# Rotary remainder term of the attention scores: two 64-row matmuls in place of two 128-row matmuls

## The chip, the cores and the metric

The kernel runs on one core of one Trainium2 chip. The metric is the time of one execution on the device in microseconds (us); the time before is the median of three runs, 1957.11 us (1955.3 to 1958.13). The engines are named as in the profile: PE is TensorE (matmuls), PEld its weight loads, DVE VectorE, ACT ScalarE, POOL GpSimd, and SP the engine whose queue issues the DMAs.

## The reference

Two batches, `s` (1024 tokens) and `p` (512 tokens), go through the same two layers: a latent attention layer and a gated MLP layer. The change touches only the scores of the attention layer, which has 8 heads:

```python
def one_block(qb):
    qn, qr = qb
    s = (jnp.einsum('bqhd,bkhd->bhqk', qn, k_nope)
         + jnp.einsum('bqhr,bkr->bhqk', qr, k_rope))
    p = jax.nn.softmax(s.astype(jnp.float32) * scale, axis=-1).astype(v.dtype)
    return jnp.einsum('bhqk,bkhd->bqhd', p, v)
```

`qn` and `k_nope` have 128 features per head. The rotary parts `qr` (per head) and `k_rope` (shared by all heads) have 64.

## The kernel before, in words

**Number format.** All large matmuls use a rounded 32-bit type (fp32r). To keep accuracy each operand is split in two: a rounded part ("hi": `qh`, `kh`, `krh`) and the remainder that the rounding left ("lo": `ql`, `kl`, `krl`). A product is then the sum of three matmuls, hi x hi, hi x lo and lo x hi, into one PSUM accumulation. `split` makes the pair: ACT rounds with a copy, DVE subtracts.

**Rotary operands.** The 64 features of the rotary query need only half of the 128 rows of the array. So the tile `qr` of a head holds its hi part in one half of the rows and its lo part in the other (hi in rows 0 to 63 for an even head, in rows 64 to 127 for an odd one). The rotary keys `krh` and `krl` are held twice, once in each half of the rows. One 128-row matmul `qr` x `krh` then gives (hi + lo) x krh, and a second one, `qr` x `krl`, gives (hi + lo) x krl.

**Scores.** `scores(i)` (lines 600 to 615) fills one PSUM tile `s` of 128 x 1024, that is two halves of 512 columns, one for each value of `j2`. For batch `s` the halves are the two key chunks of one block of 128 queries, and there are 8 heads x 8 blocks = 64 calls. For batch `p` they are two query blocks against the one key chunk, and there are 8 x 2 = 16 calls. Each half takes five matmuls of 512 columns, all on line 613: `qh` x `kh`, `qh` x `kl`, `ql` x `kh`, `qr` x `krh`, `qr` x `krl`. Every one has weights of its own (128 x 128, the query side), loaded just before it.

**What follows a score tile.** `softmax1` takes the row maximum on DVE (line 622), a scaled negative of it (line 624), and the exponential on ACT (line 628). `softmax2` normalises on DVE. `transp` makes 8 transposes on PE (line 645), ACT and DVE split the result (lines 150 and 151), and `pv` multiplies with the values on PE in matmuls of 256 columns (lines 145 to 147 with the name `o`).

**Order of work.** `main` writes the order out by hand: for each step `i` it puts the scores of `i`, the transposes of `i - 1`, the `pv` of an earlier step, and pieces that prepare the next head (`p_k`, `p_q`, `p_qr`, `p_v`), so that PE has something to do while DVE and ACT work on the softmax. `first_s` and `first_p` are the pieces ahead of each batch.

**Rotary queries.** `p_qr(p, c)` makes them for a pair of heads and a chunk of 512 tokens, in three pieces. `f1`: nine matmuls, a copy out of PSUM to `qx` on ACT (line 562), and four DMAs on SP's queue that swap 32-row strips into `qs` (line 565). `f2`: two products on DVE with the tables `cos` and `sin` (lines 569 and 570). `f3`: their sum on DVE (line 574), and for each of the two heads a rounding copy on ACT (line 578) and a subtraction on DVE (line 579) into a `qr` tile. It is called 8 times for `s` and 4 times for `p`. `begin` loads the two tables whole, once for each batch, on SP's queue (line 523).

**Buffers.** `tmp` takes a tile of 128 x 512 from a ring of five, which many steps share; a sixth user waits until the first is released.

Of the kernel before, what the change touches and what calls it, by code (L numbers as in the profile page):

```python
# [9 lines left out]
F32 = mybir.dt.float32  # L10
F32R = mybir.dt.float32r
AF = mybir.ActivationFunctionType
ALU = mybir.AluOpType
# [9 lines left out]
C = 512  # L23
# [65 lines left out]
def trunk_kernel(tc, A):  # L89
    nc = tc.nc  # L90
    pe, act, dve, pool_e = nc.tensor, nc.scalar, nc.vector, nc.gpsimd
# [3 lines left out]
    def open_pool(name, side="left", **kw):  # L95
        es_p = ExitStack()
        p = es_p.enter_context(tc.tile_pool(
            name=name, bufs=1, side=side, reuse_waits="tile", **kw))
        opened[name] = es_p
        return p  # L100
# [28 lines left out]
    st = {}  # L129


    def mm_tile(name="mm"):
        return st["ps"].tile([128, C], F32, tag=st["mm"], bufs=4, name=name)

    def big_tile(name="big"):
        return st["ps"].tile([128, 2 * C], F32, tag="big", bufs=2, name=name)

    def tmp(name="tmp", dtype=F32):
        return st["tp"].tile([128, C], dtype, tag="tmp", bufs=5, name=name)

    def mm3(out, terms):

        n = len(terms)
        for i, (lh, ll, rh, rl) in enumerate(terms):
            pe.matmul(out, lh, rh, start=(i == 0), stop=False)  # L145
            pe.matmul(out, lh, rl, start=False, stop=False)  # L146
            pe.matmul(out, ll, rh, start=False, stop=(i == n - 1))  # L147
# [135 lines left out]
    def ksl(k):  # L283
        return slice(k * 128, (k + 1) * 128)
# [228 lines left out]
    def attention(b, n_ch):  # L513

        T = n_ch * C
# [1 line left out]
        nv = 2 * n_ch  # L517

        def begin():
            ap = st["at", b] = open_pool("att" + b)  # L520
            for nm in ("cos", "sin"):
                st[nm] = ap.tile([128, T], F32, name=nm)
                nc.sync.dma_start(out=st[nm], in_=A[nm][:, :T])

        def p_k(h, c):
            def fn():
# [25 lines left out]
        def p_qr(p, c):  # L552
            cc = slice(c * C, (c + 1) * C)

            def f1():
                wh, wl = st["W"].get(("wp", p))
                ps = mm_tile()
                mm3(ps, [(wh[:, ksl(k)], wl[:, ksl(k)],
                          st["lat", b, k][0][:, cc], st["lat", b, k][1][:, cc])
                         for k in range(3)])  # L560
                qx, qs = st["qx"], st["qs"] = tmp("qx"), tmp("qs")
                act.copy(qx, ps)
                for q in range(4):
                    o = (q ^ 1) * 32
                    nc.sync.dma_start(out=qs[o:o + 32], in_=qx[q * 32:q * 32 + 32])

            def f2():
                qx, qs = st["qx"], st["qs"]
                dve.tensor_tensor(out=qx, in0=qx, in1=st["cos"][:, cc], op=ALU.mult)
                dve.tensor_tensor(out=qs, in0=qs, in1=st["sin"][:, cc], op=ALU.mult)  # L570

            def f3():
                qr = st["qx"]
                dve.tensor_tensor(out=qr, in0=qr, in1=st["qs"], op=ALU.add)
                for e in range(2):
                    t = st["at", b].tile([128, C], F32R, tag="qr", bufs=2 + n_ch, name="qr")
                    s, o = 64 * e, 64 * (1 - e)
                    act.copy(t[s:s + 64], qr[s:s + 64])
                    dve.tensor_tensor(out=t[o:o + 64], in0=qr[s:s + 64],
                                      in1=t[s:s + 64].bitcast(F32), op=ALU.subtract)  # L580
                    st["qr", 2 * p + e, c] = t
            return [(f1, ("wp", p)), (f2,), (f3,)]

        def p_v(p, i):
# [15 lines left out]
        def scores(i):  # L600
            h, blk = divmod(i, nb)
            s = big_tile("s")
            kh, kl = st["k", h]
            for j2 in range(2):
                qt, kc = (blk, j2) if n_ch == 2 else (2 * blk + j2, 0)
                c, o = divmod(qt, 4)
                o = ksl(o)
                cc = slice(kc * C, (kc + 1) * C)
                qh, ql = st["q", h, c]
                qr = st["qr", h, c]  # L610
                terms = [(qh, kh), (qh, kl), (ql, kh), (qr, st["krh", b]), (qr, st["krl", b])]
                for j, (l, r) in enumerate(terms):
                    pe.matmul(s[:, j2 * C:(j2 + 1) * C], l[:, o], r[:, cc],  # L613
                              start=(j == 0), stop=(j == 4))
            st["s", i] = s

        ns = 3 - n_ch
# [54 lines left out]
        def put(h, blk, *pc):  # L672
            pieces.setdefault(h * nb + blk, []).extend(pc)

        first = [(begin,)] + [p_k(0, c) for c in range(n_ch)] + [p_q(0, 0)] + p_qr(0, 0)
        first += [p_v(0, i) for i in range(nv)]
        for h in range(HEADS):
            p = h // 2
# [18 lines left out]
            else:  # L697
# [6 lines left out]
                elif nxt:  # L704
                    qr = p_qr(p + 1, 0)
# [4 lines left out]
        def main(weave, filler):  # L710
# [3 lines left out]
            for i in range(n + 2):  # L714
# [3 lines left out]
                if n_ch == 2 and i % 2 == 0:  # L718
                    if i < n:
                        step(lambda i=i: (scores(i), softmax1(i)))  # L720
                    if i >= 1:
                        step(lambda i=i: (transp(i - 1), transp_evac(i - 1)))
                    if i < n:
                        step(lambda i=i: softmax2(i))
                    for p in pc:
                        step(*p)
                elif n_ch == 2:
                    if i < n:
                        step(lambda i=i: (scores(i), softmax1(i), softmax2(i)))
                    if i >= 3:  # L730
                        step(lambda i=i: pv((i - 3) // 2))
                    for p in pc:
                        step(*p)
                    if i <= n:
                        step(lambda i=i: (transp(i - 1), transp_evac(i - 1)))
                else:
                    if i < n:
                        step(lambda i=i: (scores(i), softmax1(i)))
                    if i >= 2:
                        step(lambda i=i: pv(i - 2))  # L740
                    for p in pc:
                        step(*p)
                    if i < n:
                        step(lambda i=i: softmax2(i))
                    if 1 <= i <= n:
                        step(lambda i=i: (transp(i - 1), transp_evac(i - 1)))
# [838 lines left out]
```

## Time and profile before

| | |
|---|---|
| median of three runs | 1957.11 us |
| lowest and highest | 1955.3 and 1958.13 us |
| the profiled execution's own time | 1961.11 us |
| its span, first to last instruction | 1959.3 us |
| mean granted TensorE clock | 0.992 of full speed |

The profile is of one execution. Busy time of an engine is summed over its instructions. Matmuls overlap in the records: each is recorded for longer than the distance from its start to the start of the next, so what a matmul costs in a stream is read from the distance between starts.

### The profile page before, as it was taken

The page shows a single profiled execution, that of the slowest core. Times are in us where ns is not written, and L with a number is a line of the kernel's source. Part 1 is how long each engine was busy: PE and PEld are TensorE (multiplying, and loading weights), DVE is VectorE, ACT ScalarE, POOL GpSimd, SP SyncE. Part 2 cuts the span into 40 slices and gives each one's busy share as a digit, 9 for nine tenths or more (in the row PEclk, how much of TensorE's full clock was granted, in tenths as well). Part 3 has the DMA queues.
Part 4 walks back from the last instruction along what each step waited for, and adds up shares of the span by engine and source line. Part 5 has one row for each costly group of instructions (what it writes and reads, how often), then busy time and mean ns, then how long its engine had stood idle before and what let it go on. Part 6 is the DMA issues. An engine that isn't in the chain of part 4 may idle for free.

```text
span 1959.3 us, 26497 instructions
## 1 busy us (share of the span) xinstructions
PE 1918.5 (98%) x10226; PEld 1698.4 (87%) x10226; DVE 1286.6 (66%) x1958; ACT 889.0 (45%) x1382; POOL 144.3 (7%) x99
## 2 busy tenths in 40 slices
PE   8999999999998999999999999989999999999998
PEld 6888888888887888888789999978778999998887
DVE  7443777777777787549658777665655666656443
ACT  5322545444543555325544554543544454545321
POOL 5200000000011000223000000002000000000111
PEclk9999999999999999999999999999999999999999
DMA  5211000000127211676646655555575555546443
GB/s 162 86 38 57 29 13 22 17 28 17 38 68 244 85 50 60 216 257 196 201 161 226 209 193 183 173 191 186 161 245 192 177 177 183 169 135 222 168 160 103
DMA packets 118638, 269.41 MB, mean 138 GB/s; under 512 B 11888, under 2 KB 40048, under 8 KB 118512
## 3 DMA queue, kind: packets, MB, share of 16 engines
q1 hardware_dynamic: 118512, 267.73, 41.5%
q8 instruction: 80, 1.31, 0.3%
q14 instruction: 46, 0.38, 0.1%
HBM read 198.74 MB, written 65.01 MB: 135 GB/s over the span
## 4 chain that ended last, share of the span: by engine, by line
PE 88%; DVE 6%; DMA 3%; issue 1%; ACT 1%; POOL 0%; SPq 0%; POOLq 0%; DVEq 0%; ACTq 0%
PE s L613 9%; PE mm L145 7%; PE mm L146 7%; PE mm L147 7%; PE X L996 6%; PE X L997 6%; PE X L998 6%; PE mm L1257 4%; PE mm L1259 4%; PE mm L1258 4%; PE pst L645 3%; PE Z L997 3%; PE Z L996 3%; PE Z L998 3%; PE sv L1131 2%; PE o L146 2%
## 5 line engine op out<-in xcount | busy, mean ns | idle before, releaser
L63 ACT CAST w_hi<-w_raw 128x1024 fp32r<-128x1024 f32 (+3 forms) x267 | 260.6, 977 | 391.2 <-PE mm L146 102.4
L64 DVE TENSOR_TENSOR w_lo<-w_raw,w_hi 128x1024 fp32r<-128x1024 f32 (+3 forms) x267 | 303.6, 1137 | 191.5 <-ACT w_hi L63 190.8
L225 POOL TENSOR_TENSOR acc<-acc,sq 128x512 f32<-128x512 f32 x70 | 119.4, 1708 | 1444.7 <-ACT sq L223 851.2
L1257 PE MATMUL mm<-sh,w_hi 128*128 128x512 f32 (+1 forms) x416 | 155.9, 376 | 5.3 <-ACT sh L1177 5.3
L1259 PE MATMUL mm<-sh,w_lo 128*128 128x512 f32 (+1 forms) x416 | 156.1, 375 | 0.0
L1258 PE MATMUL mm<-sl,w_hi 128*128 128x512 f32 (+1 forms) x416 | 156.1, 375 | 0.0
L628 ACT ACTIVATE p<-s,sm 128x1024 f32<-128x1024 f32 (+1 forms) x96 | 93.2, 974 | 103.7 <-DVE sm L624 103.6
L150 ACT CAST pth<-pst 128x512 fp32r<-128x512 f32 x160 | 86.5, 590 | 67.4 <-PE pst L645 65.4
L145 PE MATMUL mm<-h_hi,w_hi 128*128 128x512 f32 x288 | 114.3, 397 | 1.0 <-ACT rbc L328 0.9
L146 PE MATMUL mm<-h_lo,w_hi 128*128 128x512 f32 x288 | 112.6, 391 | 0.0
L147 PE MATMUL mm<-h_hi,w_lo 128*128 128x512 f32 x288 | 112.5, 391 | 0.0
L622 DVE TENSOR_REDUCE sm<-s 128x1 f32<-128x1024 f32 (+1 forms) x80 | 97.4, 1217 | 19.5 <-PE s L613 19.4
L151 DVE TENSOR_TENSOR ptl<-pst,pth 128x512 fp32r<-128x512 f32 x160 | 104.6, 681 | 8.4 <-ACT pth L150 8.3
L1006 ACT COPY t<-X 128x384 f32<-128x384 f32 (+1 forms) x88 | 44.5, 511 | 126.9 <-PE X L998 126.0
L1257 PEld LDWEIGHTS mm<-sh,w_hi 128*128 128x128 f32 x416 | 78.9, 190 | 19.5 <-ACT sh L1177 5.7
L1258 PEld LDWEIGHTS mm<-sl,w_hi 128*128 128x128 f32 x416 | 78.9, 190 | 14.1 <-DVE sl L1178 0.2
L146 PE MATMUL o<-ptl,vh 128*128 128x256 f32 x320 | 91.1, 285 | 0.0
L1259 PEld LDWEIGHTS mm<-sh,w_lo 128*128 128x128 f32 x416 | 78.9, 190 | 14.0
L147 PE MATMUL o<-pth,vl 128*128 128x256 f32 x320 | 91.0, 284 | 0.0
L996 PE MATMUL X<-gbh,w_hi 128*128 128x384 f32 x256 | 86.0, 336 | 5.0 <-DVE uo L1096 5.0
L145 PE MATMUL o<-pth,vh 128*128 128x256 f32 x320 | 90.2, 282 | 0.0
L996 PE MATMUL X<-gah,w_hi 128*128 128x384 f32 x256 | 86.9, 339 | 0.0
(292 smaller groups left out, 5107.1 us busy)
## 6 DMA issues: line engine op xcount, KB each, us to landing
w_raw<-wbo SPq DMA_DIRECT2D x50, 512.0 KB, 3.4
w_raw<-wug SPq DMA_DIRECT2D x48, 512.0 KB, 4.4
w_raw<-sv SPq DMA_DIRECT2D x32, 512.0 KB, 3.5
su<-su SPq DMA_DIRECT2D x32, 512.0 KB, 4.4
w_raw<-su SPq DMA_DIRECT2D x32, 512.0 KB, 4.9
w_raw<-wa SPq DMA_DIRECT2D x25, 512.0 KB, 3.6
w_raw<-wv SPq DMA_DIRECT2D x24, 512.0 KB, 3.5
v2d<-c SPq DMA_DIRECT2D x48, 256.0 KB, 2.6
```

The costliest lines, as they stand in the source:

```text
L63: self.nc.scalar.copy(hi[:, :n], raw[:, :n])
L64: self.nc.vector.tensor_tensor(out=lo[:, :n], in0=raw[:, :n], in1=hi[:, :n].bitcast(F32), op=ALU.subtract)
L145: pe.matmul(out, lh, rh, start=(i == 0), stop=False)
L146: pe.matmul(out, lh, rl, start=False, stop=False)
L147: pe.matmul(out, ll, rh, start=False, stop=(i == n - 1))
L613: pe.matmul(s[:, j2 * C:(j2 + 1) * C], l[:, o], r[:, cc], start=(j == 0), stop=(j == 4))
L996: pe.matmul(ps, lh, rh, start=first, stop=False, skip_group_check=True)
L997: pe.matmul(ps, lh, rl, start=False, stop=False, skip_group_check=True)
L998: pe.matmul(ps, ll, rh, start=False, stop=last, skip_group_check=True)
L1257: pe.matmul(ps, wh[:, ksl(kk)], sh, start=(k == 0), stop=False)
L1258: pe.matmul(ps, wh[:, ksl(kk)], sl, start=False, stop=False)
L1259: pe.matmul(ps, wl[:, ksl(kk)], sh, start=False, stop=(k == 15))
```

## The change

- `scores`: each half keeps four 128-row matmuls; the fifth, `qr` x `krl`, becomes a 64-row matmul of the hi rows of the query with the same rows of `krl`. The first half uses rows 0 to 63, the second rows 64 to 127. Both are put at the end of the call, one right after the other. The product of the two remainders (lo x krl) is no longer computed.
- `p_qr`: for each pair of heads and chunk a new tile `qrx` holds the hi parts in the opposite halves of the rows (two more rounding copies on ACT in `f3`), so that a head's hi part is there in both halves.
- `cos` and `sin` are no longer loaded whole in `begin`; `f1` loads the 512 columns it needs, into a buffer of their own for `s` and into two tiles of the shared `tmp` ring for `p`.

```diff
         def begin():
-            ap = st["at", b] = open_pool("att" + b)
-            for nm in ("cos", "sin"):
-                st[nm] = ap.tile([128, T], F32, name=nm)
-                nc.sync.dma_start(out=st[nm], in_=A[nm][:, :T])
+            st["at", b] = open_pool("att" + b)
...
                 mm3(ps, [(wh[:, ksl(k)], wl[:, ksl(k)],
                           st["lat", b, k][0][:, cc], st["lat", b, k][1][:, cc])
                          for k in range(3)])
+                for nm in ("cos", "sin"):
+                    st[nm] = tmp(nm) if n_ch == 1 else st["at", b].tile(
+                        [128, C], F32, tag=nm, bufs=1, name=nm)
+                    nc.sync.dma_start(out=st[nm], in_=A[nm][:, cc])
                 qx, qs = st["qx"], st["qs"] = tmp("qx"), tmp("qs")
...
-                dve.tensor_tensor(out=qx, in0=qx, in1=st["cos"][:, cc], op=ALU.mult)
-                dve.tensor_tensor(out=qs, in0=qs, in1=st["sin"][:, cc], op=ALU.mult)
+                dve.tensor_tensor(out=qx, in0=qx, in1=st["cos"], op=ALU.mult)
+                dve.tensor_tensor(out=qs, in0=qs, in1=st["sin"], op=ALU.mult)
 
             def f3():
                 qr = st["qx"]
                 dve.tensor_tensor(out=qr, in0=qr, in1=st["qs"], op=ALU.add)
+
+                x = st["qrx", p, c] = st["at", b].tile([128, C], F32R, tag="qrx", bufs=n_ch, name="qrx")
                 for e in range(2):
                     t = st["at", b].tile([128, C], F32R, tag="qr", bufs=2 + n_ch, name="qr")
                     s, o = 64 * e, 64 * (1 - e)
                     act.copy(t[s:s + 64], qr[s:s + 64])
+                    act.copy(x[o:o + 64], qr[s:s + 64])
                     dve.tensor_tensor(out=t[o:o + 64], in0=qr[s:s + 64],
                                       in1=t[s:s + 64].bitcast(F32), op=ALU.subtract)
...
             kh, kl = st["k", h]
+            last = []
             for j2 in range(2):
...
-                terms = [(qh, kh), (qh, kl), (ql, kh), (qr, st["krh", b]), (qr, st["krl", b])]
+                terms = [(qh, kh), (qh, kl), (ql, kh), (qr, st["krh", b])]
                 for j, (l, r) in enumerate(terms):
                     pe.matmul(s[:, j2 * C:(j2 + 1) * C], l[:, o], r[:, cc],
-                              start=(j == 0), stop=(j == 4))
+                              start=(j == 0), stop=False)
+
+                rows = slice(64 * j2, 64 * j2 + 64)
+                hi = qr if j2 == h % 2 else st["qrx", h // 2, c]
+                last.append((s[:, j2 * C:(j2 + 1) * C], hi[rows, o], st["krl", b][rows, cc]))
+            for out, l, r in last:
+                pe.matmul(out, l, r, start=False, stop=True)
             st["s", i] = s
```

## Rows read from the trace of the kernel before

**Rows 1.** The page's list of engines: busy us, share of the span, instructions.
```profile
PE 1918.5 (98%) x10226; PEld 1698.4 (87%) x10226; DVE 1286.6 (66%) x1958; ACT 889.0 (45%) x1382; POOL 144.3 (7%) x99
```

**Rows 2.** Busy time by stretch of the span: attention of `s`, then of `p`.
```profile
core 0: us, PE busy (x) PEld busy (x) DVE busy (x) ACT busy (x) POOL busy (x), PEclk, DMA share, GB/s
186.00:560.00 374.00, 370.85 (x2285) 327.12 (x2285) 286.94 (x502) 192.96 (x339) 8.86 (x6) 1.00 0.09 26
...
680.00:785.00 105.00, 105.00 (x635) 92.19 (x634) 87.12 (x162) 57.22 (x125) 0.00 (x0) 1.00 0.18 57
```

**Rows 3.** What PE waited for, 180 to 790 us: total us, times, longest us.
```profile
PE ps_n L179 <- ACT sh L150: 2.1, 1, 2.1
PE ps_n L180 <- DVE sl L151: 1.9, 2, 1.6
PE pst L645 <- DVE sm L624: 1.6, 2, 1.3
PE s L613 <- ACT p L628: 1.3, 2, 1.0
```

**Rows 4.** The chain that ended last, 180 to 260 us: start us, us, what.
```profile
by line: PE s L613 36.7%; PE pst L645 12.5%; PE mm L147 10.8%; PE mm L146 10.4%; PE mm L145 10.4%; PE o L147 6.0%; PE o L146 6.0%; PE o L145 5.9%; issue 1.1%; ACT p L628 0.5%; ACTq L562 0.0%
...
233.93 2.31 PE s L613 x10
```

**Rows 5.** Instructions of the tile `s` on line 613: duration ns min/median/max, first and last start.
```profile
L613 PE MATMUL s<-kh,qh x160: 387/393/501, 189.1 to 774.5; 128*128 128x512 f32 x160
...
L613 PE MATMUL s<-krl,qr x160: 387/389/398, 193.3 to 775.5; 128*128 128x512 f32 x160
```

**Rows 6.** Timeline of one score tile and its end: start us, us, engine, instruction.
```profile
239.04 0.39 PE L613 MATMUL s<-kh,qh 128*128 128x512 f32 x1
239.04 0.19 PEld L613 LDWEIGHTS s<-kl,qh 128*128 128x128 f32 x1
239.26 0.39 PE L613 MATMUL s<-kl,qh 128*128 128x512 f32 x1
...
241.08 0.39 PE L613 MATMUL s<-krl,qr 128*128 128x512 f32 x1
241.08 0.19 PEld L145 LDWEIGHTS o<-pth,vh 128*128 128x128 f32 x1
241.31 0.28 PE L145 MATMUL o<-pth,vh 128*128 128x256 f32 x1
241.42 0.28 PE L146 MATMUL o<-ptl,vh 128*128 128x256 f32 x1
```

**Rows 7.** Timeline where transposes are followed by a score tile.
```profile
232.89 1.04 PE L645 MATMUL pst<-ident,p 128*128 128x128 f32 x8
...
233.66 0.19 PEld L613 LDWEIGHTS s<-kh,qh 128*128 128x128 f32 x1
233.68 0.48 PE L613 MATMUL s<-kh,qh 128*128 128x512 f32 x1
...
234.00 0.39 PE L613 MATMUL s<-kl,qh 128*128 128x512 f32 x1
```

**Rows 8.** Instructions of the tiles `qr` and `cos`: duration ns min/median/max.
```profile
L578 ACT CAST qr<-qx x24: 607/618/627, 191.6 to 750.5; 64x512 fp32r<-64x512 f32 x24
...
L523 SPq DMA_DIRECT2D cos<-cos x2: 372/496/621, 168.2 to 628.5; - x2
...
DMA to landing us min/median/max: 3.9/4.2/8.0
```

**Rows 9.** Timeline of the first `p_qr` and the first score tile.
```profile
178.17 0.33 SPq L55 DMA_DIRECT2D w_raw<-wh  x1
...
184.18 2.41 SPq L565 DMA_DIRECT2D qs<-qx  x4
...
189.06 0.68 DVE L569 TENSOR_TENSOR qx<-qx,cos 128x512 f32<-128x512 f32 x1
...
191.57 1.26 ACT L578 CAST qr<-qx 64x512 fp32r<-64x512 f32 x2 [1.71 <-DVE qx L574]
...
192.73 0.39 PE L146 MATMUL mm<-lat0l,w_hi 128*128 128x512 f32 x1
...
192.97 0.50 PE L613 MATMUL s<-krh,qr 128*128 128x512 f32 x1
```

## The prediction

> **What bounds the kernel now.** I read the page's list of engines first: PE is busy for 98% of the span, DVE for 66%, ACT for 45% [rows 1]. That is an average over stages, so the next view is busy time by stretch, for the two stretches in which scores are computed. In the attention of `s` PE is busy for 370.85 of 374 us, DVE for 286.94 and ACT for 192.96; in that of `p` PE is busy for 105 of 105 us, DVE for 87.12 and ACT for 57.22 [rows 2]. The granted clock is 1.00 in both, and DMA is nearly idle (0.09 and 0.18). The view of PE's waits says the same from the other side: between 180 and 790 us the four longest entries come to 6.9 us together, and two of those are norms outside the scores [rows 3]. Last, the chain that ended last: between 180 and 260 us it runs almost wholly over PE, 36.7% of it on line 613 [rows 4]. So a microsecond that PE's stream loses in these stretches is a microsecond of the time, as long as DVE keeps up.
>
> What one matmul of that stream costs is not its recorded 389 ns [rows 5] but the distance between starts. The tile of 239.04 us is followed by the first `pv` matmul at 241.31, so ten matmuls take 2.27 us; the chain puts another tile at 2.31 [rows 6, 4]. That is 0.227 to 0.231 us each; I use 0.23. The weights of a matmul begin to load when the matmul before it starts (239.04 for both) and are recorded for 0.19 us, less than 0.23, so in this stream loads are hidden [rows 6].
>
> **Part 1: two matmuls become a pair.** Line 613 has five forms of 160 matmuls, 800 in all, or ten for each of 80 score tiles [rows 5]. The count stays ten, but the last two are on different halves of the rows and write different halves of `s`, so they can run at the same time. If they overlap fully, each tile loses one slot: 80 x 0.23 = **18.4 us**. If they don't overlap, it loses nothing.
>
> A page agrees that they can: the Trainium skill, "TensorE: Matmul & The Clock Gate", Part 3, says that matmuls on different row groups run concurrently and start about 4 ns apart. By it alone the term would be an estimated 80 x (0.23 - 0.004) = 18.1 us. Every matmul of this trace is 128*128, so no row here bears it out.
>
> **Part 2: the array changes its shape twice per tile**, from 128 rows to 64 before the pair and back after it. Nothing in the trace changes shape, so this is bounded from rows. Below: nothing, if the change is made on the fly (a gain is excluded: no work is removed by it). Above: everything that is overlapped in the stream becomes visible. That is the tail of a matmul, recorded 0.39 us less the 0.23 to the next start, 0.16 us [rows 6]; and a weight load that could not run ahead. The price of the latter has a row: after eight transposes, which are too short to cover a load, the first score matmul is followed by the second after 0.32 us (233.68 to 234.00) and not 0.23, and its weights began to load only 0.02 us before it, so an uncovered load costs 0.09 us [rows 7]. Upper bound for one change of shape: 0.16 + 0.09 = 0.25 us, for two 0.50.
>
> I take **0.09 us for both together**: one load that cannot run ahead. The transposes' row is the nearest, since it is the only place where the stream goes from one kind of matmul to another, and it shows an uncovered load but no gap of a whole tail. Only one because two loads have to be made ready ahead of the pair, while after it the next load has the pair's whole 0.23 us to hide in. Whether that one load falls before the pair or between its halves makes no difference to the sum. Price: 80 x 0.09 = 7.2 us; bounds 0 and 80 x 0.50 = 40 us.
>
> **Part 3: two more rounding copies per `p_qr`.** 12 calls, 24 copies of 64 x 512; the existing ones take 0.618 us each [rows 8], so ACT gets 24 x 0.618 = 14.8 us, on an engine that is busy about half of these stretches [rows 2]. Behind them on ACT stand the exponentials and the roundings after the transposes, which PE reaches one step later. I count nothing. If that cover were gone, the place is `p`, where `f3` falls between two exponentials three times after the first: 3 x 2 x 0.618 = 3.7 us at most. The first tile of `s` is the other tight place. There the copy for `qr` starts at 191.57 and PE takes up `qr` at 192.97, 0.24 after the matmul before, so without a gap [rows 9]. Four copies instead of two end at about 191.57 + 4 x 0.62 = 194.05, and the pair, now the last of the tile, would come seven slots after 192.97 at the earliest, at 194.6: hidden.
>
> **Part 4: the tables.** Four loads go, 24 of 256 KB come, in `f1` ahead of the four `qs` DMAs on SP's queue. SP issues in some 0.5 us and a table lands in 4.2 [rows 8]. In the first call SP is free from 178.5 on, the `qs` DMAs go at 184.18 and DVE uses `cos` at 189.06 [rows 9]: a load issued by 179.5 lands by 184. The buffer of `s` is released a whole head-half earlier. For `p` the ring of five now lends four tiles from `f1` to `f2`. In the attention of `p` no other piece takes from the ring; ahead of it the slots belonged to steps PE has long passed. A weight load queued behind a table on SP has the DMA engines nearly to itself (0.09 and 0.18) [rows 2]. Nothing counted; bounded by one landing for each batch, 2 x 4.2 = 8.4 us.
>
> **Part 5: who is next.** DVE gets no work. With 64 x 0.14 = 9 us less its share in `s` becomes 286.94 / 365 = 79%, in `p` 87.12 / 102.8 = 85%. It does not become the bound.
>
> **Sum.** 18.4 - 7.2 = **11.2 us** less. The profiled execution takes 1961.1 us, 4.0 above the median of the runs; it would become 1949.9, and the median 1957.1 - 11.2 = **1946 us**.
>
> **The rivals.** *The array empties at each change of shape (slower).* The 64-row matmuls wait until the last 128-row one has left, and the next 128-row one until the pair has left. Two tails are 2 x 0.16 = 0.32 us against 0.23 saved: 0.09 x 80 = +7.2 us, 1964 us. If the loads wait as well, 2 x 0.25 - 0.23 = 0.27 us, +21.6, 1979 us. It decides from the point where the two changes together cost more than 0.23. For it: a tail of 0.16 is in flight whenever the next matmul starts, and no row shows the array being switched under it. Against it: transposes and matmuls follow each other with less than 0.1 us extra [rows 7]. The Trainium skill speaks for it: "TensorEngine Tiling (Array Packing)", Tiling Modes, says that a change of tiling mode, as against a change of tile, drains TensorE. It gives no time for that, and the trace has no such change to compare. Because of that rule I give this rival 0.28.
>
> *The pair brings nothing (the change doesn't do what it says).* The second half starts only when the first has ended, because its weights load late or because another matmul comes between: around the first tile the matmuls of `p_q` do stand between those of one tile (192.73 before 192.97) [rows 9]. Then the gain is 0 and cheap changes of shape leave 1957 us. The same time comes out if the pair overlaps and the two changes cost just about 0.23. Together 0.17.
>
> *The changes of shape cost nothing.* The whole 18.4 us, 1939 us. This is the near end of the forecast's case, not a case apart.
>
> **How the numbers follow.** The forecast's case is a pair that overlaps with changes of shape that cost at most 0.18 us together; it holds 0.55, and its own range is 1938 to 1953 us. A measurement of this kernel can tell about 0.2% from no change, 3.9 us, or 0.05 us per tile. So faster is 0.55, same 0.17, slower 0.28. The range reaches from the whole saving, 1938, past the two tails, 1964, to 1968, which takes in the late copies (3.7) on top; the case in which loads wait too, about one in ten, is left out.
>
> **What would show it.** Right: on line 613 eight 128*128 matmuls and two of 64 rows per tile, the latter starting well under 0.2 us apart, and a tile from first start to the next work in some 2.1 us; PE still busy for 98% or more of both stretches. The price of the changes is the distance from the last 128-row start to the first 64-row start, beyond 0.23, and from the second 64-row start to what follows, beyond 0.23. Parts 3 and 4 are wrong if PE waits for `qr`, `qrx` or `s` by more than the few us of now. The prediction is wrong if the two distances exceed 0.23 us in sum, or if the 64-row starts lie 0.23 apart.

## The result and the profile after

The changed kernel takes 1967.6 us (median of five runs, 1965.4 to 1973.1), the kernel before 1957.1. The ratio is **1.0057, with a 95% interval of 1.0045 to 1.0069**: slower by 0.57%, some 11 us. A second measurement on another chip, below, gave 1.0048 (1.0032 to 1.0065). The forecast was 1946 us with 0.55 on faster. The measured time lies just inside the top of the range, on the side that had 0.28.

The profiled execution of the changed kernel took 1970.89 us, its span is 1969.1 us. PE still bounds the two stretches. These are the page's list of engines and the busy time of the stretches 186 to 560 and 680 to 785 us (busy us and instructions of PE, PEld, DVE, ACT, POOL, then granted clock, DMA share, GB/s), to be read beside [rows 1, 2]:

```profile
PE 1927.2 (98%) x10226; PEld 1675.4 (85%) x10226; DVE 1289.6 (65%) x1958; ACT 903.5 (46%) x1406; POOL 144.1 (7%) x99
```

```profile
186.00:560.00 374.00, 371.44 (x2243) 304.50 (x2243) 283.56 (x490) 198.31 (x348) 6.90 (x5) 1.00 0.12 36
680.00:785.00 105.00, 105.00 (x617) 86.82 (x616) 90.07 (x165) 65.75 (x137) 0.00 (x0) 1.00 0.21 65
```

The number of matmuls is the same, 10226. PE is as full as before and got fewer of them done in the same 374 us: 2243 instead of 2285. Its weight loads were busy for 304.50 us instead of 327.12. An engine that is always "busy" and does less is the sign to look at distances between starts. The granted clock did not move. PE's waits between 180 and 800 us are those of before [rows 3], with no wait for `qr`, `qrx` or a table near the top:

```profile
PE ps_n L179 <- ACT sh L150: 3.2, 1, 3.2
PE ps_n L180 <- DVE sl L151: 2.1, 2, 1.8
PE s L618 <- ACT p L639: 1.6, 2, 1.4
```

The instructions of the tile `s` show that the change does what it says, 80 and 80 matmuls of 64 rows (64*128 stands for the rows and columns of the array that are used), and that their recorded durations say nothing of the cost (498 ns against 389):

```profile
L618 PE MATMUL s<-krh,qr x160: 387/389/499, 193.2 to 785.4; 128*128 128x512 f32 x160
...
L625 PE MATMUL s<-krl,qr x80: 492/498/503, 194.6 to 785.7; 64*128 64x512 f32 x80
...
L625 PE MATMUL s<-krl,qrx x80: 492/498/502, 194.6 to 785.7; 64*128 64x512 f32 x80
```

Now the timeline around one pair, from the last 128-row matmul of the tile into the `pv` that follows (start us, us, engine, instruction, idle before):

```profile
230.59 0.39 PE L618 MATMUL s<-kh,ql 128*128 128x512 f32 x1
230.59 0.19 PEld L618 LDWEIGHTS s<-krh,qr 128*128 128x128 f32 x1
230.81 0.39 PE L618 MATMUL s<-krh,qr 128*128 128x512 f32 x1
231.13 0.18 PEld L625 LDWEIGHTS s<-krl,qr 64*128 64x128 f32 x1 [0.35 <-issue]
231.13 0.50 PE L625 MATMUL s<-krl,qr 64*128 64x512 f32 x1
231.13 0.18 PEld L625 LDWEIGHTS s<-krl,qrx 64*128 64x128 f32 x1
231.14 0.49 PE L625 MATMUL s<-krl,qrx 64*128 64x512 f32 x1
231.56 0.19 PEld L145 LDWEIGHTS o<-pth,vh 128*128 128x128 f32 x1 [0.24 <-issue]
231.56 0.39 PE L145 MATMUL o<-pth,vh 128*128 128x256 f32 x1
231.79 0.28 PE L146 MATMUL o<-ptl,vh 128*128 128x256 f32 x1
231.90 0.28 PE L147 MATMUL o<-pth,vl 128*128 128x256 f32 x1
```

Read it by starts. The pair overlaps completely: its two starts lie 0.01 us apart. But the load for it does not begin at 230.81, when the matmul before it starts, as the loads of the plain stream do. It begins at 231.13, 0.32 us later: one slot of 0.23 (the distance between two starts in the plain stream) and 0.09 more. The pair then holds PE from 231.13 to 231.56, 0.43 us instead of 0.23. And the first `pv` matmul is followed after 0.23 us, where the next ones are 0.11 to 0.12 apart. I read the same on the way out as on the way in: the stream stops for 0.09 us beyond the slot, and only then does the load of the new shape begin, which nothing covers (0.10 to 0.11 us). Experiment 3 separates the two parts. What fills the 0.09 us the records do not show: the ends of matmuls are modelled, and the pair starts at 231.13, before the recorded end of the last 128-row matmul (230.81 + 0.39 = 231.20). All 80 pairs show these distances, with medians of 0.32 from the last 128-row start to the pair and 0.43 from the pair to what follows.

So one visit to the 64-row shape, that is the way into it and back, costs 0.09 + 0.20 + 0.10 = **0.39 us** beyond its slots (the last term is a first `pv` distance of 0.22 at the median against 0.12). Before transposes the last part is smaller: the eight transposes take 0.85 us to the next matmul (237.76 to 238.61 in the rows below) and not the 0.79 of [rows 7], so 0.35 in all. In 31 of the 80 tiles transposes follow, in 49 a `pv` or another matmul. The saved slot is 0.23: (49 x 0.39 + 31 x 0.35) / 80 - 0.23 = 0.145 us per tile, 80 x 0.145 = **11.6 us**. By the ratios the loss is 11.2 us in the first measurement and 9.4 in the second.

```profile
237.01 0.39 PE L618 MATMUL s<-krh,qr 128*128 128x512 f32 x1
...
237.33 0.50 PE L625 MATMUL s<-krl,qrx 64*128 64x512 f32 x1
...
237.76 1.09 PE L656 MATMUL pst<-ident,p 128*128 128x128 f32 x8
...
238.61 0.49 PE L145 MATMUL mm<-lat0h,w_hi 128*128 128x512 f32 x1
```

The same as a sum over the whole attention: for each PE start in the timeline, the distance to the next start, added up by kind of instruction from the first score matmul to the last (us).

| | before | changed |
|---|---|---|
| score matmuls on 128 rows, not ahead of a pair | 191.73 (800) | 135.27 (560) |
| score matmuls on 128 rows ahead of a pair | | 25.66 (80) |
| score matmuls on 64 rows | | 34.63 (160) |
| `pv`, 256 columns (`o`) | 111.33 | 114.52 |
| transposes (`pst`) | 62.76 | 63.85 |
| other matmuls of 512 columns (`mm`) | 184.00 | 186.20 |
| first to last score matmul, all kinds | 586.62 | 596.87 |

The scores themselves take 195.56 us instead of 191.73, though a slot per tile is gone. `pv` and the transposes behind them pay another 4.3. That is 8.1 us, so the price of 11.6 overstates what reaches the time by some 3.5; where these are made up I did not trace. The `mm` matmuls add 2.2 us, of which 1.6 lie between the two attentions (564.37 to 668.38 us before, 571.43 to 677.02 here), where no pair stands; that stretch takes 103.4 to 107.7 us in the profiles of this case.

### The profile page after: what moved, and what is told of

Same layout as the page of the kernel before. It is cut to its first block, busy times and chain, and to the rows that moved or that the text cites. A ratio compares the mean times of both kernels' runs of the same rounds, so it can differ in the third digit from the quotient of the medians.

```text
span 1969.1 us, 26560 instructions
## 1 busy us (share of the span) xinstructions
PE 1927.2 (98%) x10226; PEld 1675.4 (85%) x10226; DVE 1289.6 (65%) x1958; ACT 903.5 (46%) x1406; POOL 144.1 (7%) x99
## 4 chain that ended last, share of the span: by engine, by line
PE 84%; DVE 7%; DMA 5%; ACT 1%; issue 1%; POOL 0%; SPq 0%; DVEq 0%; POOLq 0%; ACTq 0%
PE s L618 7%; PE mm L145 6%; PE mm L147 6%; PE X L1007 6%; PE mm L146 6%; PE X L1009 6%; PE X L1008 6%; PE mm L1268 4%; PE mm L1269 4%; PE mm L1270 4%; PE pst L656 3%; PE Z L1008 3%; PE Z L1007 3%; PE Z L1009 3%; PE sv L1142 2%; PE o L145 2%
## 5 line engine op out<-in xcount | busy, mean ns | idle before, releaser
L145 PE MATMUL o<-pth,vh 128*128 128x256 f32 x320 | 94.8, 296 | 0.0
```

## The experiments

Ten kernels were run. The diffs are against the changed kernel; differences in us are ratios times about 1958 us.

**1. The side parts alone.** `scores` as before, the extra copies and the table loads kept.

```diff
-                terms = [(qh, kh), (qh, kl), (ql, kh), (qr, st["krh", b])]
+                terms = [(qh, kh), (qh, kl), (ql, kh), (qr, st["krh", b]), (qr, st["krl", b])]
...
-            for out, l, r in last:
-                pe.matmul(out, l, r, start=False, stop=True)
```

> The changed kernel with the scores of before: all ten matmuls of a tile on 128 rows, but the two more rounding copies and the table loads per 512 columns stay. Theory (the whole loss is in the two changes of shape around each pair): as before, 1957 us within 4. Rival (the copies, the table loads or the tighter ring of temporary tiles make the loss): about 1967 us, with waits of PE for qr, cos or temporaries.

Measured 1.0008 (0.9996 to 1.0021), +1.6 us with an interval that reaches zero. So the loss is not in the 24 copies, the 24 loads or the ring of temporary tiles; they cost at most 4 us.

**2. The pair without its overlap.** Both 64-row matmuls on rows 0 to 63.

```diff
-                rows = slice(64 * j2, 64 * j2 + 64)
-                hi = qr if j2 == h % 2 else st["qrx", h // 2, c]
+                rows = slice(0, 64)
+                hi = qr if h % 2 == 0 else st["qrx", h // 2, c]
```

> Both 64-row matmuls use rows 0 to 63, so they cannot overlap. Theory (the overlap works and is worth one slot of 0.23 us per tile): 80 x 0.23 = 18 us above the changed kernel, 1986 us, or up to 80 x 0.34 = 27 us, 1995 us, if the second one's weights cannot load ahead either. Rival (the pair brings nothing, the halves run one after another anyway): equal to the changed kernel, 1967 us.

Measured 1.0126 (1.0111 to 1.0141), 1986.5 us: 13.5 us above the changed kernel by the ratios, 16.9 us by the two profiled attentions (613.72 us from the first to the last score matmul against 596.87), where 18 was expected. A tile in the timeline:

```profile
231.25 0.39 PE L618 MATMUL s<-krh,qr 128*128 128x512 f32 x1
231.56 0.29 PEld L625 LDWEIGHTS s<-krl,qr 64*128 64x128 f32 x2 [0.35 <-issue]
231.57 0.73 PE L625 MATMUL s<-krl,qr 64*128 64x512 f32 x2
232.22 0.19 PEld L145 LDWEIGHTS o<-pth,vh 128*128 128x128 f32 x1 [0.36 <-issue]
```

The visit now lasts 0.65 us (231.57 to 232.22), the 0.43 of the overlapped pair and one slot; its median is 0.66. The overlap is real and worth its slot; the second load of the same rows hides behind the first matmul. The entry is unchanged, 0.32.

**3. Three pairs in one visit.** Six 128-row matmuls, then three pairs: nine slots again.

```diff
-                terms = [(qh, kh), (qh, kl), (ql, kh), (qr, st["krh", b])]
+                terms = [(qh, kh), (qh, kl), (ql, kh)]
...
-                last.append((s[:, j2 * C:(j2 + 1) * C], hi[rows, o], st["krl", b][rows, cc]))
-            for out, l, r in last:
-                pe.matmul(out, l, r, start=False, stop=True)
+                last.append((s[:, j2 * C:(j2 + 1) * C], hi[rows, o],
+                             [st[nm, b][rows, cc] for nm in ("krh", "krl", "krl")]))
+            for j in range(3):
+                for out, l, r in last:
+                    pe.matmul(out, l, r[j], start=False, stop=(j == 2))
```

> Per tile six 128-row matmuls and then three pairs of 64 rows, in one visit to the 64-row shape (hi x krh, hi x krl, hi x krl once more; the product lo x krh is left out, so only the time counts). Nine slots as in the changed kernel. Theory (the price is per change of shape, not per pair): a further pair costs 0.23 us like the 128-row slot it replaces, so 1967 us within 5; if within the shape loads cannot run ahead, 2 x 0.11 x 80 = 18 us more, 1985 us. Rival (a pair of 64 rows is slow by itself, 0.43 us against 0.23): 2 x 0.20 x 80 = 32 us more, 1999 us.

Measured 1.0074 (1.0059 to 1.0089), 1975.6 us: 3 us above the changed kernel by the ratios. One visit:

```profile
230.38 0.39 PE L618 MATMUL s<-kh,ql 128*128 128x512 f32 x1
230.70 0.18 PEld L627 LDWEIGHTS s<-krh,qr 64*128 64x128 f32 x1 [0.35 <-issue]
230.70 0.49 PE L627 MATMUL s<-krh,qr 64*128 64x512 f32 x1
...
230.81 0.19 PEld L627 LDWEIGHTS s<-krl,qr 64*128 64x128 f32 x1
230.81 0.19 PEld L627 LDWEIGHTS s<-krl,qrx 64*128 64x128 f32 x1
231.04 0.39 PE L627 MATMUL s<-krl,qr 64*128 64x512 f32 x1
...
231.27 0.39 PE L627 MATMUL s<-krl,qr 64*128 64x512 f32 x1
...
231.60 0.19 PEld L145 LDWEIGHTS o<-pth,vh 128*128 128x128 f32 x1 [0.37 <-issue]
```

This separates the two parts of the price. The first pair starts its successor after 0.34 us (230.70 to 231.04): its own load of 0.11, uncovered, and a slot. The next distance is 0.23 (231.04 to 231.27): within the shape both loads run ahead (230.81), and a pair costs exactly a slot. The last is 0.33: a slot and 0.10 until the old shape is through. So the price is per change of shape, not per pair. The pairs also go back and forth between the two halves of `s` at 0.23, so it is not this order, new with the change, that costs. The score matmuls sum to 197.1 us here against 195.6 in the changed kernel, and `pv` to 119.53 against 114.52, with waits for DVE that the changed kernel does not show (2.0 us for `ptl` on line 146). In the profiles the attention is thus some 6 us longer, not 3.

**4. The same matmuls in two visits.** One pair after the first half's three 128-row matmuls, two at the end.

```diff
+            for j2 in range(2):
+                (qh, kh, ql, kl, o, cc), out = last[j2][:2]
+                for j, (l, r) in enumerate([(qh, kh), (qh, kl), (ql, kh)]):
+                    pe.matmul(out, l[:, o], r[:, cc], start=(j == 0 and j2 == 0), stop=False)
+                for j in ((0,), (1, 2))[j2]:
+                    for e, (_, out, l, r) in enumerate(last):
+                        pe.matmul(out, l, r[j], start=(j == 0 and e == 1), stop=(j == 2))
```

> The same 128-row and 64-row matmuls as the run with three pairs, in another order: one pair after the first half's three 128-row matmuls, two pairs at the end, so two visits to the 64-row shape per tile in place of one. Theory: one visit more costs 0.09 (entry) + 0.20 (in the visit beyond a slot) + 0.10 (after it) = 0.39 us, 80 x 0.39 = 31 us above the run with three pairs. Rival (price per pair): no difference from the run with three pairs.

Measured 1.0185 (1.0168 to 1.0202), 1998.5 us: 22 us above experiment 3. The added visit, between two halves:

```profile
231.68 0.39 PE L623 MATMUL s<-kh,ql 128*128 128x512 f32 x1
...
232.00 0.50 PE L626 MATMUL s<-krh,qr 64*128 64x512 f32 x1
...
232.43 0.50 PE L623 MATMUL s<-kh,qh 128*128 128x512 f32 x1
...
232.77 0.39 PE L623 MATMUL s<-kl,qh 128*128 128x512 f32 x1
```

0.32, 0.43 and 0.34 us where three slots would take 0.69: 0.40 us for one visit. The distances of all score matmuls sum to 228.06 us against 197.1, 31 us more as expected; `pv` gives 4 us back (115.51 against 119.53), and its waits for DVE are gone from PE's list: probably the slower tile leaves DVE more time. The rest of the difference to the measured 22 us I did not trace.

**5 to 7. Fewer visits, the order alone, another place.** These ran beside the changed kernel on one chip.

> The changed kernel itself, beside the next three on one chip. Theory and rivals alike: some 10 to 11 us above the kernel before, ratio about 1.0055.

> In batch s the scores of two tiles are computed together and their two pairs put in one visit to the 64-row shape, so 32 visits for 64 tiles; batch p keeps 128-row remainders (no visits). Theory (0.35 to 0.39 us per visit, 0.46 us saved by its two pairs): 32 x (0.46 - 0.37) = 3 us below the run with the same order and no visits, and 13 us below the changed kernel if the order costs nothing. Rival (each pair has a price of its own): 64 x 0.15 = 10 us above the run with the same order.

> The order of the grouped run, with every remainder on 128 rows: no visit. It prices the order alone. If transposes find their softmax done in time, as before, 1957 us within 4; if not, PE waits for DVE or ACT and both grouped runs are slower by the same amount.

> The pair is put first in each tile instead of last. About 55 of 80 tiles follow transposes and there pay for an uncovered load already before the change (0.32 between the first two starts instead of 0.23). Theory (each change of shape is an emptying of about 0.09 us and an uncovered load of about 0.11): those tiles pay the load at entry once, not twice, so 55 x 0.31 + 25 x 0.39 = 27 us of price instead of 30, some 3 us below the changed kernel. Rival (the price is one lump per change, wherever it stands): equal to the changed kernel within 1.

The edit of the grouped run, in short (the order control puts `krl` back among the 128-row terms):

```diff
-        def scores(i):
+        def scores(*ii):
...
-                        step(lambda i=i: (scores(i), softmax1(i)))
+                        step(lambda i=i: (scores(i, i + 1), softmax1(i)))
...
-                        step(lambda i=i: softmax2(i))
+                        step(lambda i=i: (softmax1(i + 1), softmax2(i)))
...
-                        step(lambda i=i: (scores(i), softmax1(i), softmax2(i)))
+                        step(lambda i=i: softmax2(i))
```

The changed kernel again, without an edit: 1.0048 (1.0032 to 1.0065). The order alone: 1.0040 (1.0026 to 1.0054), +7.8 us, so the order was not free. Grouped: 1.0085 (1.0068 to 1.0102), 9 us above the order alone where 3 us below was expected. The visit is as forecast, two pairs for one price, 0.32 into it and 0.34 + 0.32 through it:

```profile
230.98 0.39 PE L623 MATMUL s<-krh,qr 128*128 128x512 f32 x1
231.30 0.49 PE L631 MATMUL s<-krl,qr 64*128 64x512 f32 x1
...
231.64 0.39 PE L631 MATMUL s<-krl,qr 64*128 64x512 f32 x1
...
231.96 1.09 PE L661 MATMUL pst<-ident,p 128*128 128x128 f32 x8
```

The score matmuls do take 4.9 us less than in the order control (183.76 against 188.69). But with the pairs at the very end both tiles are ready only then, the softmax of the first starts 1.8 us later (its maximum on DVE starts 4.39 us after the first score matmul at the median, against 2.61 in the order control), and PE waits more further on. PE's waits in the grouped run, then in the order control:

```profile
PE o L146 <- DVE ptl L151: 9.2, 10, 2.2
PE s L623 <- ACT p L644: 3.4, 1, 3.4
PE o L145 <- ACT pth L150: 3.1, 7, 0.7
```

```profile
PE s L622 <- ACT p L637: 6.3, 5, 2.2
...
PE o L145 <- ACT pth L150: 1.1, 3, 0.6
```

`pv` and the transposes together grow by 11.3 us against the control (126.18 + 71.21 against 119.00 + 67.06). So the theory's price held and its saving was lost to new waits. The total, 9 us above the order alone, is close to the 10 us of the rival. Taken alone it would have spoken for a price per pair; the timeline and the sum of the score matmuls speak against it.

The pair first in the tile:

```diff
+                out = s[:, j2 * C:(j2 + 1) * C]
+                pe.matmul(out, hi[rows, o], st["krl", b][rows, cc], start=True, stop=False)
+                last.append((out, o, cc, [(qh, kh), (qh, kl), (ql, kh), (qr, st["krh", b])]))
+            for out, o, cc, terms in last:
+                for j, (l, r) in enumerate(terms):
+                    pe.matmul(out, l[:, o], r[:, cc], start=False, stop=(j == 3))
```

It measured 1.0092 (1.0073 to 1.0112), 9 us above the changed kernel, where 3 us below was expected. Two things went against it. After transposes the entry costs more, not less: 0.96 us from the first of eight transposes to the pair against 0.79 to a 128-row matmul [rows 7], 0.17 more, and the pair still pays its load (0.43 to the next start).

```profile
236.22 1.03 PE L654 MATMUL pst<-ident,p 128*128 128x128 f32 x8
...
237.18 0.50 PE L619 MATMUL s<-krl,qr 64*128 64x512 f32 x1
237.61 0.19 PEld L623 LDWEIGHTS s<-kh,qh 128*128 128x128 f32 x1 [0.24 <-ACT pth L150]
```

And the first tile can no longer begin without the rotary operands: the first score matmul starts at 192.5 us instead of 189.3. With the attention itself 3.2 us longer than in the changed kernel beside it (601.07 against 597.86) this makes 6.4 of the 9 us. So "0.09 to empty" holds after matmuls of 512 columns; after transposes it is about twice that, and why is open.

**8. One visit for two tiles in the old order.** The first tile of two does its own pair and opens the second tile's accumulation with the second pair.

```diff
+            if i % 2 == 0:
+                st["s", i], st["s", i + 1] = big_tile("s"), big_tile("s")
...
+                    pe.matmul(out, l[:, o], r[:, cc], start=(j == 0 and i % 2 == 0),
+                              stop=(j == 3 and i % 2 == 1))
+            if i % 2 == 0:
+                for e in range(2):
+                    for j2 in range(2):
+                        c, o, cc, out = half(i + e, j2)
+                        rows = slice(64 * j2, 64 * j2 + 64)
+                        hi = st["qr", h, c] if j2 == h % 2 else st["qrx", h // 2, c]
+                        pe.matmul(out, hi[rows, o], st["krl", b][rows, cc], start=(e == 1), stop=(e == 0))
```

> The order of the work as in the kernel before; the first tile of each two computes its own pair at its end and, in the same visit, the pair with which the second tile's accumulation begins. 40 visits for 80 tiles, and no softmax waits for a later tile. Theory (0.35 us per visit where transposes follow, up to 0.39 otherwise; 0.46 saved by the two pairs): 40 x (0.46 - 0.37) = 4 us below the run with the side parts alone, so about 1956 us, within 0.2% of the kernel before, and 12 us below the changed kernel. Rival (a price per pair, or waits of the softmax as in the grouped run): 10 us above the kernel before.

Measured **0.9985 (0.9976 to 0.9994)**, 1956.5 us against 1960.1 beside it: by the ratios 2.9 us faster than the kernel before, and 12 to 14 us faster than the changed one in its two measurements. It is the fastest version that keeps the whole product of the changed kernel. A shared visit:

```profile
237.49 0.40 PE L620 MATMUL s<-krh,qr 128*128 128x512 f32 x1
237.82 0.50 PE L628 MATMUL s<-krl,qrx 64*128 64x512 f32 x1
...
238.16 0.39 PE L628 MATMUL s<-krl,qrx 64*128 64x512 f32 x1
...
238.48 1.09 PE L658 MATMUL pst<-ident,p 128*128 128x128 f32 x8
```

The two pairs take 0.66 us (237.82 to 238.48), two slots and 0.20. The score matmuls sum to 187.05 us (144.79 + 12.92 + 29.34), 4.7 less than before. So the price of a visit is borne out, but that the total came out as worked out is in part luck. The transposes (65.1 us against 62.8), `pv` (112.3 against 111.3) and the other matmuls take the 4.7 us back, and the profiled executions need the same 586.4 us from the first score matmul to the last (189.07 to 775.47 before, 189.44 to 775.82 here). Where the 2.9 us arise is open: the profiled spans differ after the last score matmul, where no edit is, 1183.8 us before against 1179.6 here, and the other profiles of this case have 1180.0 to 1186.1 there.

**9. No pair at all.** The eight 128-row matmuls alone.

```diff
-                              start=(j == 0), stop=False)
+                              start=(j == 0), stop=(j == 3))
...
-            for out, l, r in last:
-                pe.matmul(out, l, r, start=False, stop=True)
```

> The changed kernel without the hi x krl term: eight 128-row matmuls per tile, no pair, no change of shape (the term is left out of the result). It prices a slot of PE in the whole kernel. Theory (PE bounds these stretches, a slot of 0.23 us is 0.23 us of the time): 80 x 2 x 0.23 = 37 us below the run with the side parts alone, about 1922 us. Rival (DVE or ACT take over as PE's stream gets shorter): clearly less, 20 us or so, with waits of PE for the softmax.

Measured 0.9863 (0.9846 to 0.9880), 27 us less than before and 28 less than the side parts alone, not 37. About three quarters of two slots per tile arrive in the time. The rest turns into waits of PE on the softmax; its waits between 180 and 830 us now have, beside the old ones:

```profile
PE s L618 <- ACT p L633: 4.4, 7, 2.0
...
PE pst L650 <- DVE p L641: 2.3, 4, 1.6
```

## Why the prediction was wrong

**The bound (right, with a limit).** PE's stream sets the time of the attention. Experiment 9 adds that the stock of slack is finite: a slot is worth its 0.23 us while the tile stays about as long as it was, and less beyond.

**Part 1 (right).** The pair overlaps, starts 0.00 to 0.01 us apart, and saves one slot per tile (experiment 2). The Trainium skill, "TensorE: Matmul & The Clock Gate", Part 3, puts these starts about 4 ns apart; the trace agrees.

**Part 2 (the step that failed).** "0.09 us for both together: one load that cannot run ahead." Measured: 0.39 us, or 0.35 before transposes, which is within the bounds of 0 and 0.50 but about four times the value taken, and across the 0.23 at which the sign turns. Three things were wrong in it. No load runs ahead over a change of shape, neither into the pair nor out of it, so two loads are uncovered and not one. Having 0.23 us of the pair to hide in does not help the load after it, since that load begins only when the next matmul does (231.56 for both). And the stream does stop at each change, by about 0.09 us. The transposes' row [rows 7] was the wrong neighbour: there the load is late behind short matmuls (0.1 us apart, a load is recorded for 0.19), with no change of shape involved. It priced a load, and nothing of the stop.

**The rival that came true.** "The array empties at each change of shape", in its form where the loads wait as well. It set 0.16 + 0.09 = 0.25 us per change, +21.6 us in all. Measured are about 0.09 + 0.11 = 0.20 per change, less into transposes, and 9.4 to 11.2 us in all. The tail in the records (0.39 less 0.23) overstates the stop. The Trainium skill's rule that a change of tiling mode drains TensorE ("TensorEngine Tiling (Array Packing)", Tiling Modes) fits the trace, which shows a stop of 0.09 us at each change but not the emptying itself. I gave this rival no more than 0.28, because I took the load price from an unlike row for the price of the whole change. That the time lies inside the range is luck: the top of 1968 us was put together from two tails of 0.16 us and late copies, the stops measured 0.09 and the copies were not late, and the form in which loads wait had been left out of the range.

**Parts 3 to 5 (right within the measurement).** Copies, tables and ring cost 1.6 us with an interval of -0.8 to 4.1, and DVE did not become the bound (283.56 and 90.07 us busy in the two stretches).

## What to carry to other kernels

When two small matmuls are to share the array, count the changes of shape and not only the slots: here one visit cost 0.35 to 0.39 us, more than the 0.23 that one pair of 512 columns saves, so a visit needs at least two pairs to gain, and two gained at most 2.9 us here. Gather them where nothing downstream has to wait for the later one, as in experiment 8 and not as in experiment 5. And where the trace of before has no instance of an operation, a nearby row that is slow for another reason is no price for it: keep the forecast as wide as the bounds.

## What the runs showed of the hardware that was not expected

- Over a change between 128*128 and 64*128 in a stream of 512-column matmuls the next load begins 0.09 us after the last matmul's slot and is uncovered for 0.11 us, in both directions (0.32 us into the visit, 0.33 at its end, 0.34 to the next start in experiments 3 and 4). Within the shape both halves' loads run ahead, and a pair of 64-row matmuls costs one slot of 0.23 us (experiment 3).
- From transposes into the 64-row shape the stop was 0.17 us longer than from transposes into a 128-row matmul (experiment 7).
- An accumulation can begin with a 64-row matmul and go on with 128-row ones, and the reverse (experiments 7 and 8). The shared visit of experiment 8, which does both, takes 0.33 us to enter and 0.66 to pass through, as that of experiment 5 does (0.32 and 0.66).
